# A list schedule of a decoder layer's token mixers with measured task times, and five gate tiles among its filler

## The chip, the cores and the metric

One core of a Trainium2 chip runs the whole layer as one launch. The metric is the device time of a run in microseconds (us), the median of several runs. The engines are named as in the profile: PE (TensorE matmul), PEld (its weight load), DVE (VectorE), ACT (ScalarE), POOL (GpSimd), SP (SyncE, which here issues the DMAs).

## The reference

```python
for i in range(DEPTH):                      # DEPTH 1, x is 512 x 1024
    h = h + FFN_HALF * _swiglu(_rmsnorm(h, norm_ffn1[i]), ffn1_gate[i], ffn1_up[i], ffn1_down[i])
    u = _rmsnorm(h, norm_mix[i])
    (nq, kc, vc, ksl, vsl, kwn, vwn, ng, sq, sk, sv, ga, gb) = jnp.split(u @ w_in[i], pts, axis=-1)
    ...
    o_a = _nsa(nq, kc, vc, ksl, vsl, kwn, vwn, ng, positions, ...)   # 8 heads: compressed, selected, window
    o_b = _banded_attention(sq, sk, sv, SWA_WINDOW, swa_sinks[i]).reshape(B, S, SWA_Q_W)
    merged = jax.nn.sigmoid(ga) * (o_a @ w_branch_a[i]) + jax.nn.sigmoid(gb) * (o_b @ w_branch_b[i])
    h = h + merged @ w_out[i]
    h = h + FFN_HALF * _swiglu(_rmsnorm(h, norm_ffn2[i]), ffn2_gate[i], ffn2_up[i], ffn2_down[i])
return _rmsnorm(h, norm_final)
```

## The kernel before

Every matrix product is made of three matmuls in fp32r: each weight block and each activation is split into a high part and a low part (`whi`, `wlo`; `uh`, `ul`). A weight block (`raw`, 128 rows x 8 x 128) comes by DMA from the SP queue into one of four raw buffers; ACT writes `whi` (L93) and DVE or POOL writes `wlo` (L97, "a split"). Both go into a ring of four slots. A split in halves is 128x512.

The stages are: first FFN, mixers, merge, second FFN. In the mixers (`layer`, from the line `plan = Schedule(...)`) all steps are tasks: projections of `u` (`project`, 256 columns for two weight blocks at a time), their ropes and transposes, the compression of keys and values (`compress`), and the attention of 8 sliding-window units and then 24 units of the sparse attention (`attend`: scores on PE, mask and minimum on DVE, exponentials on ACT, "weighing" of the probabilities by the inverse sum on DVE or POOL, transposes and value products on PE). Each attention step is a chain over PE, DVE and ACT.

The matmuls of projections and compression are *filler* (`filler`, rank 9000): they stand in one chain on PE, and the schedule puts them where PE has no attention step to do. Behind the projections the filler goes on with the tiles of the merge gates that depend on `u` alone (`gate_early`): eight tiles of gate A and `GB_EARLY` tiles of gate B. A gate tile is 24 matmuls of 512 columns; its result is copied by ACT to `turn_a` and written to DRAM (`zd`) from the SP queue.

`Schedule.run` (L199) is the planner, and it runs while the program is built: of all ready tasks it takes the one with the smallest key, adds its time in us to the clock of its engine, and emits its instructions. A task may name two engines with a time for each. A buffer ring (`Ring`) holds a task back until a buffer is free by the plan. What it makes is a fixed order of instructions on each engine; on the chip an engine waits wherever an instruction's input is late.

The merge then goes over eight tiles `d`: it loads the stored gate tiles (`load_z`, a DMA and a product by `r_b` on POOL), computes those tiles of gate B that are not stored (24 matmuls and a product on DVE), makes the two branch products (12 matmuls each), multiplies on DVE, adds on POOL, and splits the sum for the product with `w_out`.

## Time and profile before

| | |
|---|---|
| runs | 1142.55, 1146.53, 1146.96 us, median 1146.53 |
| profiled execution | 1143.02 us, of which the span of its instructions is 1141.3 us |
| PE busy | 1117.3 us, 98% of the span |
| DVE, ACT, POOL busy | 652.8, 440.9, 132.1 us |
| mixers | from about 388 to 640 us of the span |
| merge, with the product with `w_out` | from 640 us |

A matmul is shown from its start to the modelled end of its pipeline, while the next one starts before that end. So a PE that is shown as busy is not always at its peak, and a short wait can lie within the busy time. The table of stretches gives the busy time of each engine within a stretch and the granted share of TensorE's clock (PEclk).

### The profile page before, as it was taken

How to read it: one execution, taken by the hardware profiler on the slowest of the kernel's cores; microseconds unless marked ns; L12 is line 12 of the kernel's file. 1: busy time of each engine (PE TensorE's matmuls, PEld its weight loads, DVE VectorE, ACT ScalarE, POOL GpSimd, SP SyncE). 2: the span in 40 equal slices, each digit the busy share in tenths (PEclk: the TensorE clock that was granted, in tenths of full speed). 3: DMA queues.
4: the chain of work that ended last, by engine and by line, in shares of the span. 5: the costliest groups of instructions: out<-in, count | busy, mean ns of one | idle time of the engine just before them, and what ended most of it. 6: DMA issues, size and time to landing. Idle time of an engine off the chain costs nothing.

```text
span 1141.3 us, 14617 instructions
## 1 busy us (share of the span) xinstructions
PE 1117.3 (98%) x5583; PEld 939.8 (82%) x5583; DVE 652.8 (57%) x1227; ACT 440.9 (39%) x858; POOL 132.1 (12%) x137
## 2 busy tenths in 40 slices
PE   8999999999999999999999899999999999999997
PEld 6888888888888999888888688888888888888875
DVE  4564345643547599999889644565443344433453
ACT  4432122321323356757777533333222133222432
POOL 0100000000005221422112222240000000000001
PEclk9999999999999999999999999999999999999999
DMA  7233333233225442333111345423333332333221
GB/s 226 76 111 111 92 93 111 78 107 111 74 84 155 131 111 76 83 103 84 47 38 37 101 134 157 139 88 116 97 110 94 92 101 84 111 93 92 75 73 74
DMA packets 198287, 113.34 MB, mean 99 GB/s; under 512 B 4996, under 2 KB 191944, under 8 KB 198216
## 3 DMA queue, kind: packets, MB, share of 16 engines
q1 hardware_dynamic: 197416, 111.33, 34.0%
q8 instruction: 44, 0.72, 0.3%
q10 hardware_dynamic: 800, 1.07, 0.3%
q14 instruction: 27, 0.22, 0.1%
HBM read 105.83 MB, written 6.55 MB: 98 GB/s over the span
## 4 chain that ended last, share of the span: by engine, by line
PE 88%; DVE 8%; issue 1%; ACT 1%; DMA 0%; SPq 0%; POOLq 0%; DVEq 0%; ACTq 0%
PE acc L250 32%; PE s L250 28%; PE o L250 25%; DVE wlo L97 2%; PE tp L1244 2%; DVE s L1150 1%; DVE pts L1259 1%; PE tp L250 0%; DVE osum L1287 0%; DVE pbuf L1181 0%; PE tp L870 0%; DVE h L504 0%; DVE pbuf L1179 0%; DMA w_in<-in_ffn_up_dram 0%; PE tp L1365 0%
## 5 line engine op out<-in xcount | busy, mean ns | idle before, releaser
L97 DVE TENSOR_TENSOR wlo<-raw,whi 128x1024 fp32r<-128x1024 f32 (+3 forms) x221 | 242.6, 1127 | 28.3 <-ACT whi L93 27.3
L93 ACT CAST whi<-raw 128x1024 fp32r<-128x1024 f32 (+3 forms) x223 | 189.8, 890 | 131.2 <-PE acc L250 53.8
L250 PE MATMUL acc<-uh,whi 128*128 128x512 f32 x296 | 117.1, 396 | 0.0
L250 PE MATMUL acc<-ul,whi 128*128 128x512 f32 x296 | 115.7, 391 | 0.0
L250 PE MATMUL acc<-uh,wlo 128*128 128x512 f32 x296 | 115.7, 391 | 0.0
L250 PE MATMUL s<-uh,whi 128*128 128x512 f32 x280 | 109.4, 391 | 0.0
L250 PE MATMUL s<-ul,whi 128*128 128x512 f32 x280 | 109.2, 390 | 0.0
L250 PE MATMUL s<-uh,wlo 128*128 128x512 f32 x280 | 109.0, 389 | 0.0
L250 PE MATMUL o<-uh,whi 128*128 128x512 f32 x256 | 101.2, 395 | 0.6 <-ACT uh L553 0.6
L250 PE MATMUL o<-ul,whi 128*128 128x512 f32 x256 | 100.1, 391 | 0.0
L250 PE MATMUL o<-uh,wlo 128*128 128x512 f32 x256 | 99.8, 390 | 0.0
L253 ACT CAST G<-g 128x512 fp32r<-128x512 f32 x44 | 27.3, 621 | 186.2 <-DVE g L469 186.2
L250 PE MATMUL acc<-G,whi 128*128 128x512 f32 x280 | 87.6, 394 | 0.0
L250 PE MATMUL s<-G,whi 128*128 128x512 f32 x228 | 70.3, 389 | 0.0
L250 PE MATMUL o<-G,whi 128*128 128x512 f32 x228 | 70.2, 389 | 0.0
L250 PE MATMUL acc<-whi,uh 128*128 128x256 f32 x224 | 64.7, 289 | 2.0 <-DVE v L829 2.0
L250 PEld LDWEIGHTS acc<-uh,wlo 128*128 128x128 f32 x296 | 55.6, 188 | 12.3 <-DVE wlo L97 0.4
L250 PE MATMUL acc<-wlo,uh 128*128 128x256 f32 x224 | 63.6, 284 | 1.6 <-DVE wlo L97 1.6
L465 ACT ACTIVATE s<-z 128x512 f32<-128x512 f32 x44 | 27.9, 633 | 95.7 <-DVE z L463 95.7
L250 PEld LDWEIGHTS acc<-uh,whi 128*128 128x128 f32 x296 | 55.7, 188 | 10.8 <-issue 0.2
L250 PEld LDWEIGHTS acc<-ul,whi 128*128 128x128 f32 x296 | 55.8, 188 | 10.6
L250 PE MATMUL acc<-whi,ul 128*128 128x256 f32 x224 | 63.3, 283 | 0.0
(298 smaller groups left out, 2115.3 us busy)
## 6 DMA issues: line engine op xcount, KB each, us to landing
raw<-in_ffn_gate_dram SPq DMA_DIRECT2D x42, 512.0 KB, 3.9
raw<-in_ffn_up_dram SPq DMA_DIRECT2D x42, 512.0 KB, 5.1
raw<-in_ffn_down_dram SPq DMA_DIRECT2D x38, 512.0 KB, 4.3
raw<-in_w_in_dram SPq DMA_DIRECT2D x32, 512.0 KB, 4.7
raw<-in_w_out_dram SPq DMA_DIRECT2D x8, 512.0 KB, 4.5
raw<-in_ffn_down_dram SPq DMA_DIRECT2D x8, 384.0 KB, 4.0
zd<-turn_a SPq DMA_DIRECT2D x9, 256.0 KB, 2.1
z<-zd SPq DMA_DIRECT2D x9, 256.0 KB, 2.6
```

Of the source, the lines that this page charges most:

```text
L93: self.nc.scalar.copy(self.place(i)[0][:, k0:k1], self.raw[i][:, k0:k1])
L97: engine.tensor_tensor(lo, self.raw[i][:, k0:k1], f32(hi), op=OP.subtract)
L250: tensor.matmul(out, lhsT, rhs, start=start, stop=stop)
L253: scalar.copy(hi, src)
L465: scalar.activation(s, z, AF.Silu)
L1150: vector.tensor_tensor_reduce(b.view[:, j], b.view[:, j], u.mask, 1.0, u.least(hd), OP.add, OP.min, u.m[:, hd:hd + 1])
L1244: tensor.transpose(ps[:w, hd], u.p[:, hd, kb * w:kb * w + w], ident)
L1259: vector.tensor_tensor(p.lo, flat(b.ps)[:w], f32(p.hi), op=OP.subtract)
```

## The change

The planner's time for nearly every task is replaced, by values that are mostly longer. The fixed delay of 0.15 us between engines becomes one that depends on the engine that comes before and on whether POOL comes after. The key of the choice was "end by the plan, less the task's time on its faster engine"; it is now the start by the plan, then the rank, then the task's time, so that a task with two engines goes to the one that is free first. And gate B's tiles 0, 2, 4, 6 and 7 are filler of the mixers, where it was tile 0 alone; tiles 1, 3 and 5 stay in the merge. No arithmetic changes.

```diff
-GB_EARLY = 1
+GB_EARLY = 0, 2, 4, 6, 7
...
-    SEM = 0.15
+    SEM = {"pe": 0.2, "act": 0.05, "dve": 0.05, "pool": 0.08, "sp": 2.0}
+    TO_POOL = 0.1
...
-                least = min(t.us.values())
                 for e, us in t.us.items():
-                    start = max(at, self.clock[e])
-                    key = (start + us - least, t.rank, t.seq)
+                    start = max(at, self.clock[e], *(end + self.delay(p, e) for p, end in t.sources))
+                    key = (start, t.rank, us, t.seq)
...
-    plan_in(C_GB, GB_EARLY * 128)
+    for d in GB_EARLY:
+        plan_in(C_GB + d * 128, 128)
...
-                    x = prepped[i, half] = task(either(us), low, (t, last_low[0] if half else None), rank=PREP)
+                    x = prepped[i, half] = task(either(us, 0.16), low, (t, last_low[0] if half else None), rank=PREP)
...
-        for d in range(KD + GB_EARLY):
+        for d in (*range(KD), *(KD + d for d in GB_EARLY)):
             gate_early(d)
...
-                    x = task(("act", per * (0.24 + u.n * 0.83e-3)), lambda u=u, hs=hs, b=b: exps(u, hs, b), (x,),
+                    x = task(("act", per * (0.24 + u.n * 1.08e-3)), lambda u=u, hs=hs, b=b: exps(u, hs, b), (x,),
...
-                if d >= GB_EARLY:
+                if d not in GB_EARLY:
                     gates_z[1] = mp.tile([128, S], F32, name="z1")
...
-                elif d + 1 < GB_EARLY:
+                if d + 1 in GB_EARLY:
                     zb = load_z(KD + d + 1)
```

Three places show how the order moves. The rows name output and inputs with their buffer numbers; the line numbers of the changed kernel are four or five higher.

DVE, at the projection of the first keys and values (`acc_3423` before, `acc_3496` now): `turn_a` and `turn_b` are its rope, and `v` is the last step that reads its PSUM bank. Before:

```order
L764 TENSOR_TENSOR turn_a_3574<-acc_3423,cos_87 128x256
L767 TENSOR_TENSOR turn_b_3575<-acc_3423,sin_88 128x4x32 x2
L97 TENSOR_TENSOR wlo_71<-raw_3325,whi_70 128x512
L97 TENSOR_TENSOR wlo_71<-raw_3342,whi_70 128x512
L97 TENSOR_TENSOR wlo_71<-raw_3325,whi_70 128x512
L1287 TENSOR_TENSOR osum_3621<-o_3529,up_3566 64x256 x2
L97 TENSOR_TENSOR wlo_71<-raw_3342,whi_70 128x512
L829 SCALAR_TENSOR_TENSOR v_2556<-acc_3423,rcol_2635,v_2556 128x2x64 x2
```

Now:

```order
L769 TENSOR_TENSOR turn_a_3664<-acc_3496,cos_87 128x256
L772 TENSOR_TENSOR turn_b_3665<-acc_3496,sin_88 128x4x32 x2
L787 TENSOR_TENSOR turn_a_3664<-turn_a_3664,turn_b_3665 128x256
L834 SCALAR_TENSOR_TENSOR v_2556<-acc_3496,rcol_2635,v_2556 128x2x64
L834 SCALAR_TENSOR_TENSOR v_2556<-acc_3496,rcol_2635,v_2556 128x2x64
```

Four splits and an `osum` that stood between the rope and `v` are gone from there; the second half of the rope (L787), which POOL did, is on DVE.

POOL, in the projections, behind the four steps of `compress_in` (`ql` and `G<-osum` are low parts, as `wlo` is). Before:

```order
L861 TENSOR_TENSOR ql_3023<-turn_a_2993,ql_3023 128x8x64
L782 TENSOR_TENSOR turn_a_3025<-turn_a_3025,turn_b_3026 128x512
L97 TENSOR_TENSOR wlo_71<-raw_3078,whi_70 128x512
L861 TENSOR_TENSOR ql_3367<-turn_a_3293,ql_3367 128x8x64
L1292 TENSOR_TENSOR G_76<-osum_3397,G_76 128x256
L782 TENSOR_TENSOR turn_a_3435<-turn_a_3435,turn_b_3436 128x256
L782 TENSOR_TENSOR turn_a_3574<-turn_a_3574,turn_b_3575 128x256
L1179 TENSOR_SCALAR pbuf_2560<-pbuf_2560,c_3499 128x256 x4
```

Now:

```order
L866 TENSOR_TENSOR ql_3250<-turn_a_3223,ql_3250 128x8x64
L1297 TENSOR_TENSOR G_76<-osum_3288,G_76 128x256
L97 TENSOR_TENSOR wlo_71<-raw_3081,whi_70 128x512 x2
L97 TENSOR_TENSOR wlo_71<-raw_3103,whi_70 128x512
L97 TENSOR_TENSOR wlo_71<-raw_3133,whi_70 128x512
L1297 TENSOR_TENSOR G_76<-osum_3467,G_76 128x256
L1184 TENSOR_SCALAR pbuf_2560<-pbuf_2560,c_3345 128x256 x2
L97 TENSOR_TENSOR wlo_71<-raw_3372,whi_70 128x512 x2
L97 TENSOR_TENSOR wlo_71<-raw_3393,whi_70 128x512
L97 TENSOR_TENSOR wlo_71<-raw_3418,whi_70 128x512 x2
```

Splits of weights have taken the place of rope sums and weighings on POOL: over the whole program POOL has 30 half splits where it had 2, and DVE 50 where it had 70 (eight more halves come with the gate tiles). Of the weighings in blocks of 384 and 512 columns, POOL keeps 1 of 20.

PE, at the end of the mixers: `o` with `pts` are value products, `tp` transposes of probabilities, `acc` with `uh` or `ul` filler, and `acc` with `G` the first branch product of the merge. Before:

```order
L250 MATMUL acc_5635<-uh_74,wlo_71 128x512
L1244 MATMUL tp_5796<-ident_79,pbuf_2560 128x128 x4
L250 MATMUL o_5808<-pts_2561,v_2556 128x512 x2
L1244 MATMUL tp_5813<-ident_79,pc_5742 32x128 x4
L250 MATMUL o_5808<-pts_2561,v_2556 128x512 x2
L250 MATMUL o_5808<-pts_2561,vc_2549 128x512
L250 MATMUL acc_5852<-G_76,whi_70 128x512 x2
```

Now (from the same last-but-one transposes on; then follow eight more filler matmuls and `acc_5988<-G`):

```order
L254 MATMUL acc_5891<-uh_74,wlo_71 128x512
L1249 MATMUL tp_5930<-ident_79,pc_5850 32x128 x4
L254 MATMUL acc_5891<-uh_74,whi_70 128x512
L254 MATMUL acc_5891<-ul_75,whi_70 128x512
L254 MATMUL acc_5891<-uh_74,wlo_71 128x512
L254 MATMUL o_5905<-pts_2561,v_2556 128x512 x2
L254 MATMUL acc_5891<-uh_74,whi_70 128x512
L254 MATMUL acc_5891<-ul_75,whi_70 128x512
L254 MATMUL acc_5891<-uh_74,wlo_71 128x512
L254 MATMUL o_5905<-pts_2561,vc_2549 128x512
L254 MATMUL acc_5891<-uh_74,whi_70 128x512
```

The filler had run out before the last five steps of the attention; now three filler matmuls stand between each two of them and nine behind the last.

## Rows read from the trace of the kernel before

**Rows 1.** The page's first part: busy time, share of the span, instructions.

```profile
PE 1117.3 (98%) x5583; PEld 939.8 (82%) x5583; DVE 652.8 (57%) x1227; ACT 440.9 (39%) x858; POOL 132.1 (12%) x137
```

**Rows 2.** Busy time by stretch: its length, then each engine (instructions), PEclk, DMA.

```profile
core 0: us, PE busy (x) PEld busy (x) DVE busy (x) ACT busy (x) POOL busy (x), PEclk, DMA share, GB/s
388.00:520.00 132.00, 126.46 (x1039) 122.85 (x1038) 120.21 (x338) 87.22 (x239) 32.57 (x32) 1.00 0.34 89
520.00:630.00 110.00, 109.96 (x606) 90.34 (x604) 98.05 (x299) 80.72 (x244) 22.75 (x32) 1.00 0.18 53
630.00:640.00 10.00, 6.87 (x31) 4.10 (x30) 7.90 (x25) 6.26 (x23) 2.90 (x3) 1.00 0.24 81
640.00:650.00 10.00, 10.00 (x38) 8.17 (x38) 4.80 (x7) 5.01 (x8) 3.05 (x3) 0.83 0.32 105
```

**Rows 3.** PE's waits from 388 to 645 us: total, times, longest.

```profile
PE o L250 <- DVE pts L1259: 2.1, 3, 0.9
PE acc L250 <- DVE v L829: 2.0, 1, 2.0
PE acc L250 <- DVE wlo L97: 1.6, 2, 1.0
...
PE tp L250 <- DVE sqacc L995: 0.6, 2, 0.4
```

**Rows 4.** PE in order of time: start, length, matmul, [idle before, releaser].

```profile
457.04 0.28 PE L250 MATMUL acc<-whi,G 128*128 128x256 f32 x1
457.16 0.28 PE L250 MATMUL acc<-wlo,G 128*128 128x256 f32 x1
459.49 0.36 PE L250 MATMUL acc<-whi,uh 128*128 128x256 f32 x1 [2.05 <-DVE v L829]
...
636.13 0.49 PE L250 MATMUL o<-pts,v 128*128 128x512 f32 x1 [0.91 <-DVE pts L1259]
...
639.52 0.50 PE L250 MATMUL o<-pts,vc 64*128 64x512 f32 x1 [0.92 <-DVE pts L1259]
639.95 1.22 PE L250 MATMUL acc<-G,whi 128*128 128x512 f32 x2
...
643.67 0.63 PE L250 MATMUL acc<-G,whi 128*128 128x512 f32 x2
...
647.09 0.39 PE L250 MATMUL s<-uh,whi 128*128 128x512 f32 x1
647.32 0.39 PE L250 MATMUL s<-ul,whi 128*128 128x512 f32 x1
```

**Rows 5.** DVE in order of time, ahead of PE's longest wait.

```profile
454.90 2.43 DVE L97 TENSOR_TENSOR wlo<-raw,whi 128x512 fp32r<-128x512 f32 x3
457.26 0.84 DVE L1287 TENSOR_TENSOR osum<-o,up 64x256 f32<-64x256 f32 x2
...
458.74 0.60 DVE L829 SCALAR_TENSOR_TENSOR v<-acc,rcol,v 128x128 fp32r<-128x128 f32 x2
```

**Rows 6.** DVE's groups by shape, 388 to 640 us: busy us, mean ns of one.

```profile
L97 DVE TENSOR_TENSOR wlo<-raw,whi 128x512 fp32r<-128x512 f32 x56 | 42.9, 816 | 2.7 <-ACT whi L93 2.6
...
L1181 DVE TENSOR_SCALAR pbuf<-pbuf,c,gate 128x512 f32<-128x512 f32 x7 | 3.8, 547 | 0.3
...
L1181 DVE TENSOR_SCALAR pbuf<-pbuf,c,gate 128x384 f32<-128x384 f32 x5 | 2.4, 480 | 0.3
```

**Rows 7.** DVE's splits (L97), 388 to 641 us: ns min/median/max.

```profile
L97 DVE TENSOR_TENSOR wlo<-raw,whi x60: 411/682/1799, 388.8 to 601.8; 128x512 fp32r<-128x512 f32 x56, 128x256 fp32r<-128x256 f32 x4
```

**Rows 8.** POOL's groups by shape, 388 to 720 us.

```profile
L1319 POOL TENSOR_TENSOR z<-z,r_b 128x512 f32<-128x512 f32 x9 | 11.8, 1306 | 31.8 <-DMA z<-zd 18.4 <-DVE z L1332 12.4 <-PE tp L1244 1.0
...
L97 POOL TENSOR_TENSOR wlo<-raw,whi 128x512 fp32r<-128x512 f32 x2 | 2.6, 1320 | 16.6 <-ACT whi L93 16.6
```

**Rows 9.** POOL's waits, 370 to 660 us: total, times, longest.

```profile
POOL G L1292 <- ACT G L1291: 41.0, 7, 16.8
```

**Rows 10.** The page's DMA issues: KB each, us to landing.

```profile
z<-zd SPq DMA_DIRECT2D x9, 256.0 KB, 2.6
```

More of the change, by code (lines that the diff above doesn't have):

```diff
@@ L221, in run @@
                 n.left -= 1
-                n.ready = max(n.ready, end + (0.0 if e in n.us and len(n.us) == 1 else self.SEM))
+                n.sources.append((e, end))
+                n.ready = max(n.ready, end)
                 if n.left == 0:
@@ L751, in emit @@
                                 mm(ps[:, t], ul[:, j, ts], hi[:, :, j], False, j == KD - 1)
-                        x = filler(0.65, emit, (prepped[first, k // 4], prepped[first + 1, k // 4]),
+                        x = filler(0.725, emit, (prepped[first, k // 4], prepped[first + 1, k // 4]),
                                    take=[(r_acc, b)] if t == 0 and k == 0 else ())
@@ L831, in v_low @@
                                                     op0=OP.mult, op1=OP.subtract)
-                v_ready[ty, t0] = task(("dve", 0.5), v_low, (x1, vh), give=[(r_acc, b)], rank=-1)
+                v_ready[ty, t0] = task(("dve", 0.6), v_low, (x1, vh), give=[(r_acc, b)], rank=-1)
                 def dup():
@@ L870, in turn @@
                             tensor.transpose(p[:, hd], s.ql[:, t, hd], ident_r)
-                    tt = task(("pe", 0.25), turn, (lo,), take=[(r_tp, bank)],
+                    tt = task(("pe", 0.33), turn, (lo,), take=[(r_tp, bank)],
                               give=[(r_ql, key)] if t else (), rank=-1)
                     q_ready[slot0 + t0 + t] = task(
-                        ("act", 0.5), lambda t=t, bank=bank: scalar.copy(G[:, slot0 + t0 + t], f32(flat(bank.ps))),
+                        ("act", 0.59), lambda t=t, bank=bank: scalar.copy(G[:, slot0 + t0 + t], f32(flat(bank.ps))),
                         (tt, *wait), give=[(r_tp, bank)], rank=-1)
@@ L963, in emit @@
                         mm(ps, blk[ix][:, r * 8 + i], lo[:, :, i], False, i == 7)
-                x = filler(0.43, emit, (prepped[first, j // 4], prepped[first + 1, j // 4], *ins),
+                x = filler(0.48, emit, (prepped[first, j // 4], prepped[first + 1, j // 4], *ins),
                            take=[(r_acc, b)] if j == 0 else ())
@@ L987, in poly @@
                 vector.tensor_tensor(gy, gy, gx, op=OP.mult)
-            x = task(("dve", 1.0), poly, (x,), give=[(r_tp, bank)], rank=-1)
+            x = task(("dve", 1.6), poly, (x,), give=[(r_tp, bank)], rank=-1)
             x = task(("act", 0.25), lambda: scalar.activation(gy, gy, AF.Tanh, scale=math.sqrt(2 / math.pi)), (x,),
@@ L995, in product @@
                 vector.scalar_tensor_tensor(gy, gy, 1.0, gx, op0=OP.add, op1=OP.mult)
-            x = task(("dve", 0.5), product, (x,), rank=-1)
+            x = task(("dve", 0.7), product, (x,), rank=-1)
             bank2 = Bank()
@@ L1055, in emit @@
                     mm(ps, lo[:, k], uh[:, k], False, k == KD - 1)
-                x = filler(0.65, emit, (prepped[first, k // 4],), take=[(r_acc, b)] if k == 0 else ())
+                x = filler(0.685, emit, (prepped[first, k // 4],), take=[(r_acc, b)] if k == 0 else ())
             used[first] = x
@@ L1062, in out @@
                 nc.sync.dma_start(zd[d], z)
-            x = task(("act", 0.5), out, (x,), take=[(r_turn, b)], give=[(r_acc, b)], rank=-1)
+            x = task(("act", 0.6), out, (x,), take=[(r_turn, b)], give=[(r_acc, b)], rank=-1)
             task(("sp", 2.0), lambda: None, (x,), give=[(r_turn, b)], rank=-1)
@@ L1259, in low @@
                         vector.tensor_tensor(p.lo, flat(b.ps)[:w], f32(p.hi), op=OP.subtract)
-                    hi = task(("act", 0.5), high, (t_last,), rank=rank, take=[(r_pt, p)])
-                    lo = task(("dve", 0.62), low, (hi,), rank=rank, give=[(r_tp, b)])
+                    hi = task(("act", 0.59), high, (t_last,), rank=rank, take=[(r_pt, p)])
+                    lo = task(("dve", 0.69), low, (hi,), rank=rank, give=[(r_tp, b)])
                     def value(u=u, kb=kb, p=p):
@@ L1270, in value @@
                         mm(o, u.v(kb), p.lo, False, kb == u.nb - 1 and u.last)
-                    v_last = task(("pe", 0.22 if u.ty == 2 else 0.43), value, (v_last, lo, *u.v_ready), rank=rank,
+                    v_last = task(("pe", 0.42 if u.ty == 2 else 0.455), value, (v_last, lo, *u.v_ready), rank=rank,
                                   give=[(r_pt, p)],
@@ L1320, in load_z @@
                 return z
[L1322 removed]
+            za, zb = load_z(0), load_z(KD)
             for d in range(KD):
@@ L1327, in layer @@
                     za = load_z(d + 1)
-                if d >= GB_EARLY:
+                if d not in GB_EARLY:
                     gates_z[1] = mp.tile([128, S], F32, name="z1")
```

33 lines of the change are left out of this document (17 added, 16 removed).

## The prediction

> **What bounds the kernel now.** I began with the page's first part: PE is busy for 1117.3 of 1141.3 us [rows 1], so no change that only moves work can bring more than some 24 us, and moving matmuls from the merge into the mixers moves as much PE time as it takes away. What is to be had are PE's waits, and the second question is where they lie. The stretches answer it [rows 2]: PE is idle for 132.00 - 126.46 = 5.54 us in the projections (388 to 520 us), 0.04 us in the 110 us of sparse attention behind them, and 3.13 us in the last 10 us of the mixers; and in the 10 us after that the granted clock is 0.83. In the projections DVE is busy for 120.21 of 132 us, 91%. Then the list of waits [rows 3]: seven lines, 11 waits, 8.5 us in sum, and every one of them is put down to DVE. So the mixers are held up by DVE, off and on, in a stage that PE would otherwise set.
>
> How much that costs is read from the starts of matmuls [rows 4]. Filler matmuls of 256 columns start 0.12 us apart (457.04, 457.16) though each is shown for 0.28; the next one starts at 459.49, which is 2.33 - 0.12 = 2.21 us late where the row says 2.05. Each wait is thus some 0.16 us longer than its row, 1.8 us for 11 of them. The clock: the nine matmuls of 512 columns from 639.95 to 643.67 take 3.72 us, while at full clock they start 0.23 apart (647.09, 647.32), which makes 2.05; so 1.67 us are lost there at the lower of the two levels, 1.2 GHz, after three waits of 0.9 us each in the 4 us ahead. The sum of all that can be won is 5.54 + 0.04 + 3.13 + 1.8 + 1.67 = 12.2 us, of it some 6.8 in the projections and 5.3 at the end. Waits shorter than 0.16 us show in no row; I allow 2 us for them at the low end of the range, nothing in the sum.
>
> **The change part by part.** *The longest wait.* PE waits at 457.16 for the PSUM bank that the step `v` frees, and DVE got to `v` late: between the rope and `v` stood three splits (2.43 us), an `osum` pair (0.84) and a fourth split [rows 5], about 4 us of work. In the new order one rope sum stands there instead, as the rows of DVE's order ahead show. That wait, 2.2 us, should go. It is what the longer task times do: the old plan had DVE far ahead of where the chip has it, and put splits in its way that the chip could not do in that time.
>
> *DVE's load.* In the new order DVE has 20 half splits fewer (50 for 70): 20 x 0.816 = 16.3 us less [rows 6]. It takes over 11 weighings of 384 columns and 8 of 512 from POOL: 11 x 0.480 + 8 x 0.547 = 9.7 us more [rows 6], nearly all in the sparse attention; and some ten smaller ones, in the sliding-window units, at no more than 0.48 each, 4.8 us at most. Of the extra splits on POOL about 20 stand in the projections. So DVE's work there goes from 120.2 to about 120.2 - 16.3 + 4.8 = 109 us of at least 126.5 us of PE work, 86% at most. In the sparse attention it goes from 98.05 + 7.90 to some 116 us, but there PE's stretch grows by four gate tiles of 24 matmuls at 0.227 us (2.05 / 9), 21.8 us, from 120 to 142: 82%. In the stretch from 520 to 630 us DVE was at 98.05 of 110, 89%, and PE idle for 0.04 us [rows 2]. Both stretches would now be below that.
>
> *What stays of the 6.8 us in the projections.* Bounds: nothing (as in the stretch at 89%), and all of it, if DVE were still late at each place. I take 1.5 us, much nearer to the first since the share falls below that row's.
>
> *The end of the mixers.* Before, the filler had run out, and the last steps stood back to back on PE. Now 3 filler matmuls (0.68 us) stand between each two of the last steps, and 9 (2.04 us) behind the last one. The three waits of 0.9 us there [rows 3, 4] shrink to 0.24 each, 0.7 us in all; without waits I see no reason for the clock to fall, so its 1.67 us go too. What is late next is the first use of the last unit's `G`: 12 matmuls of the other branch stood ahead of it before and no wait is listed there [rows 3]; now 21 do. I keep 0.7 of the 5.3 us (bounds 0 and, if the attention ends 2 us later than planned so that filler runs dry again, 3).
>
> *The four gate tiles.* 96 matmuls of 512 columns leave the merge and enter the mixers: zero. Each brings an ACT copy and a 256 KB write on SP's queue, and in the merge a load and a product on POOL (1.306 us [rows 8]) for a product that DVE no longer does; none of them is work of PE. SP's queue stands in order: a write waits for its copy, and weight loads stand behind it, but these run three blocks (over 8 us of PE work) ahead. In the merge a tile whose gates are both stored takes PE 24 x 0.227 = 5.45 us. Tiles 6 and 7 come one after the other: tile 7's gates are loaded only when tile 5 is split, in 2.6 us [rows 10]; then two POOL products (2.6 us) stand ahead of the sums of tiles 6 and 7 on POOL's queue (estimated at a product's 1.3 each), and a split on ACT and DVE ends it (estimated at twice 0.68): 9.2 us behind tile 5's split, which by the same values comes some 3.4 us behind its last branch product. PE runs on through 10.9 us of branch products and 21 matmuls of `w_out` (4.8 us) before it needs tile 7's sum: 15.7 against 12.6. Bounds 0 and 3 us, if the locks told of below hit each step; I take 0.
>
> *Waits that are new.* 28 more half splits stand on POOL, at 1.320 us each where DVE's median is 0.682 [rows 7, 8]. PE's filler waits for both. A split is made two to four blocks ahead; a pair of blocks feeds 96 matmuls of a projection, 11.5 us. That covers 0.64 us, but the blocks of `compress` feed 16 matmuls, 1.9 us, for four half splits. Bounds 0 and 0.64 x 20 = 13 us; I take 0.5.
>
> Sum: 12.2 - 1.5 - 0.7 - 0 - 0.5 = 9.5 us, and 1143.0 - 9.5 = 1133.5 us on the scale of the profiled execution. The runs shown lie from 0.5 below to 3.9 above that execution; I take 1134.
>
> **A rule that speaks against it.** Where a DVE split met a POOL sum it took up to 1.799 us for a median of 0.682 [rows 7], and the mean of all 56 is 0.816 [rows 6], 7.5 us in sum. The Trainium skill, SBUF — State Buffer, section "Who interferes with whom", says that a DVE instruction with two SBUF inputs and a GpSimd instruction that reads SBUF lock each other out for a whole instruction. By that rule the longest split of the trace is one that waited out a POOL sum, and each of the new POOL splits can do the same to DVE. What that would give is the first rival.
>
> **The rivals.** *POOL's splits take back what DVE gains.* A split that is held up loses 1.799 - 0.682 = 1.1 us [rows 7]. If each of the 20 extra POOL splits in the projections costs DVE that much, its work there is 109 + 22 = 131 us, over the 128 us or so that the stretch would take, and it is the bound again: the 6.8 us stay, the end is still won (4.6), and 0.5 to 1 us of late splits comes on top. 1143.0 - 4 = 1139. For it: rows 7. Against it: over all 56 splits the mean lies only 0.13 us above the median [rows 6, 7], so most did not meet a POOL step at its start.
>
> *The schedule only moves the waits.* The plan has no lock in it and its times are means; DVE is late at other steps, and the filler that was to cover the end is used up earlier. Then half of 12.2 us is won: 1137. Against it: where DVE's share was 89% there was no wait.
>
> *Slower: splits queued behind POOL's `G` steps.* POOL works in order, and it waited 41.0 us for ACT ahead of seven `G` steps, 16.8 at the longest [rows 9]. In the new order ten such steps are on POOL and splits stand right behind most of them. If an attention unit ends late, the splits behind its `G` step are late, and with them PE's filler, which ends later units. At 2 us (as the wait at 457 us) for each of eight of them, 16 us come back: 1143.0 - 12.2 + 16 + 1.5 = 1148. It decides from 9.5 us in sum, 1.2 for each. Against it: the splits run blocks ahead of their use.
>
> **How the numbers follow.** Forecast 0.70 (1129 to 1137); POOL's splits 0.14 (1139); moved waits 0.10 (1137); slower 0.06 (1148). The low end is all 12.2 us and 2 us of hidden waits: 1129, less 1 since a run can lie below the profiled one; the high end takes in the first two rivals and the runs' scatter of 3.9 us: 1143. About 0.5%, 5.7 us, is what a measurement of this kernel can tell from no change. Against the median of 1146.53 that is 1140.8, against the profiled execution 1137.3. All of the forecast and half of the moved waits come out as faster, 0.76 with a bit of the first rival; the rest of these two as the same, 0.18; slower 0.06.
>
> **What would show it.** Right: PE's idle time from 388 to 520 us below 2 us, no wait of 2 us for `v`; the granted clock 1.00 in each stretch up to the merge; the filler's last matmuls behind the last value product with waits of under 0.3 us; DVE's share below 88% in the projections; the merge without a wait of PE. Wrong: waits of PE for POOL's splits; DVE's mean split over 0.9 us; a wait of PE at `w_out` for `mh`; or waits of PE for DVE as long as before at other steps.

## The result, and the profile after

The changed kernel takes 1156.16 us (median of 4 runs, 1155.72 to 1156.53) where the kernel before takes 1146.62; the ratio is 1.0091, with a 95% interval of 1.0068 to 1.0114. It is slower, by 0.9%, where 1134 us and faster was forecast. The profiled execution took 1155.72 us, its span is 1154.0 against 1141.3 [rows 1]: 12.7 us to be found.

The page's first part after the change, busy time, share of the span and instructions, which answers to [rows 1]:

```profile
PE 1121.1 (97%) x5583; PEld 940.9 (82%) x5583; DVE 663.9 (58%) x1226; ACT 442.1 (38%) x866; POOL 157.4 (14%) x142
```

Five stretches of it: length, then busy time of each engine (instructions), granted clock, DMA share, GB/s. They answer to [rows 2]; with four more gate tiles among the filler the mixers now end at about 665 us, not at 641.

```profile
388.00:520.00 132.00, 121.10 (x985) 116.22 (x984) 116.61 (x306) 80.02 (x214) 47.39 (x36) 1.00 0.33 89
520.00:660.00 140.00, 139.37 (x759) 115.06 (x758) 126.14 (x358) 98.21 (x298) 28.55 (x30) 1.00 0.21 63
...
670.00:680.00 10.00, 6.09 (x16) 4.10 (x15) 3.15 (x5) 3.39 (x6) 4.98 (x4) 0.67 0.35 118
680.00:730.00 50.00, 50.00 (x221) 41.17 (x220) 25.56 (x36) 18.16 (x32) 19.50 (x15) 1.00 0.58 172
730.00:740.00 10.00, 8.02 (x28) 5.86 (x27) 4.83 (x6) 4.78 (x7) 2.95 (x3) 0.83 0.79 231
```

PE is idle for 10.90 us in the projections, where it was 5.54; the merge has two holes, at 670 and at 730 us, each with a lower granted clock. PE's waits from 388 to 790 us (total, times, longest), which answer to [rows 3]:

```profile
PE acc L254 <- DVE wlo L97: 3.9, 4, 1.6
PE s L254 <- ACT whi L93: 3.9, 1, 3.9
PE tp L254 <- DVE sqacc L977: 1.7, 2, 1.5
PE tp L1249 <- DVE c L1173: 1.6, 1, 1.6
PE o L254 <- ACT whi L93: 1.5, 1, 1.5
PE acc L254 <- DVE v L834: 1.4, 1, 1.4
PE tp L807 <- ACT pbuf L911: 1.3, 1, 1.3
...
```

Two kinds make up most of it: waits for DVE in the projections as before, only more, and waits for ACT's weight casts (`whi`), which were not there. No row of PE names a split on POOL; its weight load (PEld) waited for one twice, 2.4 us in all.

Since such rows miss the slow clock behind a wait, this text measures PE's **lost time**: for each matmul, the time to the next one's start less what its shape takes at full clock (0.230 us for 512 columns, 0.121 for 256, 0.110 for all others), summed by stage. The 32 matmuls of 384 columns need more than 0.110, which puts the same 2.0 us into each row of the column of the mixers; differences are free of it. The stages are the projections (388 to 520 us), the rest of the mixers (up to the first matmul of the merge that reads `G`), the merge (up to the first that reads `mh`), and `w_out`. The expectations below count the end of the mixers from 620 us on: 5.3 before, 2.7 after the change, 21.2 with the schedule alone. The last two columns are counts of POOL's instructions from 388 to 680 us; `osum` is the start of the last `osum` on DVE, which is where attention ends.

```
kernel             time us  ratio   lost: proj. mixers merge w_out   osum  POOL splits, weighings
before             1146.6   -              5.5   10.2   0.7   0.5    641       2     42
after              1156.2   1.0091        12.5    6.7   7.8   3.0    664      32     13
e1_sched_only      1167.7   1.0196        12.4   25.3   0.4   0.5    664      28     10
e2_gates_only      1150.4   1.0045         7.3    6.4   8.0   1.9    648       3     43
e3_dve_splits      1164.0   1.0158         7.0   23.2   3.9   3.1    679       0      8
e4_next_first      1153.3   1.0061        15.0    6.7   3.2   1.9    668      32     13
e5_old_key         1166.0   1.0183        16.9   17.7   3.0   3.1    682      13      5
e6_gates_clean     1140.0   0.9956         5.6    6.4   1.1   1.6    646       3     43
e7_after_clean     1147.9   1.0032        12.5    6.8   1.0   1.6    665      32     13
e8_beside_tt       1154.3   1.0078        15.1   10.9   1.2   0.5    652       2     42
e9_beside_set      1144.0   0.9987         4.8   10.5   0.7   0.5    640       2     42
e11_same_delay     1157.7   1.0116        20.0    9.9  -0.5   0.5    656      28     52
e12_weigh_dve      1160.7   1.0143         8.9   22.7   1.6   0.5    658       5      0
e13_before_pool    1159.8   1.0125        22.9   10.0   1.1   0.5    659      22     30
e14_emit_dve       1156.2   1.0090        11.5    6.9   8.6   3.1    664       0     13
e15_all_three      1140.1   0.9964         6.7    5.4   0.1   1.6    656       0     64
```

Ratios are to the runs of before on the same chip; their intervals are no wider than 0.0046. After less before is 7.0 in the projections, -3.5 in the rest of the mixers, 7.1 in the merge and 2.5 at `w_out`: 13.1 us, and -0.3 in the first FFN, against 12.7 of span.

### The profile page after: what moved, and what is told of

The parts are those of the page before. It is cut to its first block, busy times and chain, and to the rows that moved or that the text cites. A ratio compares the mean times of both kernels' runs of the same rounds, so it can differ in the third digit from the quotient of the medians.

```text
span 1154.0 us, 14622 instructions
## 1 busy us (share of the span) xinstructions
PE 1121.1 (97%) x5583; PEld 940.9 (82%) x5583; DVE 663.9 (58%) x1226; ACT 442.1 (38%) x866; POOL 157.4 (14%) x142
## 4 chain that ended last, share of the span: by engine, by line
PE 86%; DVE 8%; ACT 3%; issue 1%; DMA 1%; POOL 0%; SPq 0%; POOLq 0%; DVEq 0%; ACTq 0%
PE acc L254 31%; PE s L254 26%; PE o L254 26%; DVE wlo L97 3%; PE tp L1249 2%; ACT whi L93 1%; DVE s L1155 1%; DVE pts L1264 1%; PE tp L254 0%; DVE pbuf L1184 0%; ACT pbuf L1163 0%; DVE turn_b L772 0%; DVE turn_a L769 0%; DMA z<-zd 0%; DVE h L509 0%
## 5 line engine op out<-in xcount | busy, mean ns | idle before, releaser
L97 DVE TENSOR_TENSOR wlo<-raw,whi 128x1024 fp32r<-128x1024 f32 (+3 forms) x195 | 231.2, 1209 | 30.2 <-ACT whi L93 29.1
L254 PE MATMUL acc<-uh,whi 128*128 128x512 f32 x352 | 139.9, 397 | 0.0
L254 PE MATMUL acc<-uh,wlo 128*128 128x512 f32 x352 | 137.6, 391 | 0.0
L254 PE MATMUL acc<-ul,whi 128*128 128x512 f32 x352 | 137.5, 391 | 0.0
L254 PE MATMUL s<-uh,whi 128*128 128x512 f32 x232 | 91.9, 396 | 3.9 <-ACT whi L93 3.9
L254 PE MATMUL s<-ul,whi 128*128 128x512 f32 x232 | 91.5, 394 | 0.0
L254 PE MATMUL s<-uh,wlo 128*128 128x512 f32 x232 | 91.3, 394 | 0.0
L254 PE MATMUL s<-G,whi 128*128 128x512 f32 x268 | 82.6, 389 | 0.0
L254 PEld LDWEIGHTS acc<-uh,wlo 128*128 128x128 f32 x352 | 66.1, 188 | 14.6 <-DVE wlo L97 0.6
L254 PEld LDWEIGHTS acc<-uh,whi 128*128 128x128 f32 x352 | 66.3, 188 | 13.1 <-issue 0.7
L254 PEld LDWEIGHTS acc<-ul,whi 128*128 128x128 f32 x352 | 66.3, 188 | 12.6
L254 PE MATMUL acc<-G,whi 128*128 128x512 f32 x232 | 71.4, 389 | 0.0
```

What stands on the lines that cost most here:

```text
L97: engine.tensor_tensor(lo, self.raw[i][:, k0:k1], f32(hi), op=OP.subtract)
L254: tensor.matmul(out, lhsT, rhs, start=start, stop=stop)
```

## The hole at the start of the merge

ACT of the changed kernel in order of time (start, length, line, [idle before, releaser]) from 664 to 676 us, then POOL, SP's queue and PE there:

```profile
665.56 0.59 ACT L1066 COPY turn_a<-acc 128x512 f32<-128x512 f32 x1 [0.29 <-PE acc L254]
666.16 1.28 ACT L1341 ACT_TABLE_LOAD   x1
673.21 0.63 ACT L1341 ACTIVATE z<-z 128x512 f32<-128x512 f32 x1 [5.76 <-POOL z L1324]
673.75 1.03 ACT L93 CAST whi<-raw 128x1024 fp32r<-128x1024 f32 x1
```

```profile
670.70 3.71 POOL L1324 TENSOR_TENSOR z<-z,r_b 128x512 f32<-128x512 f32 x3 [10.81 <-DMA z<-zd]
```

```profile
666.17 0.32 SPq L1067 DMA_DIRECT2D zd<-turn_a  x1
666.60 2.16 SPq L1323 DMA_DIRECT2D z<-zd  x2
```

```profile
670.57 0.39 PE L254 MATMUL o<-G,wlo 128*128 128x512 f32 x1
674.83 0.79 PE L254 MATMUL s<-uh,whi 128*128 128x512 f32 x1 [3.87 <-ACT whi L93]
675.42 0.63 PE L254 MATMUL s<-ul,whi 128*128 128x512 f32 x1
676.09 0.79 PE L254 MATMUL s<-uh,wlo 128*128 128x512 f32 x1
...
677.11 0.63 PE L254 MATMUL s<-ul,whi 128*128 128x512 f32 x1
677.53 0.63 PE L254 MATMUL s<-uh,wlo 128*128 128x512 f32 x1
```

Read it from the top. The last stored gate tile now ends the mixers: its copy stands at 665.56 us and its write at 666.17, behind the merge's first matmul, where before the copy (633.87) was 6 us ahead of that matmul (639.95 [rows 4]). The merge's first load of a gate tile stands behind that write on SP's queue; POOL's products follow at 670.70 and the first sigmoid at 673.21. None of that is what PE needs: the next matmul wants a weight block whose cast is written behind the sigmoid in ACT's order, and so ACT sits idle for 5.76 us ahead of a cast whose input is there. Behind the wait three matmuls start some 0.6 us apart and the next ones 0.43, not 0.23: the granted clock, 1.00 up to 672 us, is 0.50 from 674 to 680. Something like it stands at 731 us:

```profile
727.88 2.55 POOL L1324 TENSOR_TENSOR z<-z,r_b 128x512 f32<-128x512 f32 x2 [4.28 <-DVE z L1344]
730.39 1.29 POOL L1346 TENSOR_TENSOR z<-z,z 128x512 f32<-128x512 f32 x1
```

```profile
731.71 0.62 ACT L257 CAST mh<-z 128x512 fp32r<-128x512 f32 x1 [5.36 <-POOL z L1346]
732.24 0.62 ACT L1341 ACTIVATE z<-z 128x512 f32<-128x512 f32 x1
732.77 1.03 ACT L93 CAST whi<-raw 128x1024 fp32r<-128x1024 f32 x1
```

Here POOL's sum for tile 6 stands behind the two products for tile 7, whose loads were issued at 725.01, right behind the split (724.29) that is the last to read tile 5's buffer. ACT waits for that sum ahead of its `mh` cast, and the weight cast for `w_out` stands behind this cast and a sigmoid of tile 7.

## The experiments

**One part of the change at a time.** The schedule alone has `GB_EARLY = 0,` in the changed kernel. The other kernel has the planner, key and times of before with the tuple below and the loops that read it:

```diff
-GB_EARLY = 1
+GB_EARLY = 0, 2, 4, 6, 7
```

> The new list schedule alone: GB_EARLY holds only tile 0, as before the change, so gate tiles 2, 4, 6 and 7 are computed in the merge again. Theory, two separate causes: (1) the new order puts the weight splits on POOL and costs TensorE about 7 us in the projections (idle of 388 to 520 us 10.9 against 5.5 before); (2) the five early gate tiles cost two waits in the merge and at w_out, 7.1 and about 4 us, because weight casts stand behind sigmoids on ACT, while they win the waits at the end of the mixers, 6.6 us. With (1) alone the projections keep an idle time of 10 to 12 us, the two waits in the merge are gone, and the end of the mixers waits again as before or more: 1156 - 11 + 6.6 = 1152 us (1149 to 1155). Rival, the gate tiles carry the whole loss: 1142 to 1147.

> The five early gate tiles alone, with the planner and the task times of before. By the theory of two causes the projections idle 5 to 6 us as before, the waits at the end of the mixers go (6.6 us) and the two waits of the merge and of w_out are as after the change (11 us): 1146.6 + 11 - 6.6 = 1151 us (1148 to 1154). Rival, the loss is all in the new order: 1138 to 1142.

The schedule alone took 1167.7 us, beyond both theories; the gates alone 1150.4, as the theory of two causes had it. The table shows why the first missed: attention ends at 664 us with the new schedule whether the gate tiles are in it or not, 23 us later than before. Without them filler is out early and PE loses 25.3 us in the rest of the mixers; with them 22 us of gate matmuls (four more tiles, 96 matmuls at 0.23) lie over just that delay. One half of the change hides what the other costs, and a comparison of before and after alone would not have shown it.

**The merge.** First the next block ahead of the sigmoid:

```diff
                 for z, x in zip(gates_z[::-1], (b_in, a_in)):
+                    w = W.next()
                     scalar.activation(z, z, AF.Sigmoid)
                     ps = acc(False)
-                    mm3(ps.rearrange("p (t c) -> p t c", t=4), W.next(), x, 4)
+                    mm3(ps.rearrange("p (t c) -> p t c", t=4), w, x, 4)
```

> The changed kernel with one edit in the merge loop: the next weight block's cast and split are written ahead of the sigmoid instead of behind it. Theory, in ACT's order the casts stand behind sigmoids that wait for the stored gate tiles: the waits of 3.9 us at 670 us with its slow clock after it (7.1 together) and of about 4 us at w_out go or fall below 1.5 each, 1156 - 9 = 1147 us (1145 to 1150). Rival, TensorE waits there for the transfers and products of the gate tiles themselves, or for the weight loads behind them: the waits move by a product or two and the time stays at 1154 to 1157.

Then with `bufs=3` for the tiles `z0` and `z1` as well, once on the changed kernel and once on the gate tiles with the planner of before:

> The changed kernel with both edits of the merge: the next block's cast and split ahead of each sigmoid, and three buffers for z0 and z1. With the first edit alone (1153.3 us) two waits of about 2.3 us each were left where a cast stands behind a sigmoid whose gate tile came late. Theory, the load starts late because a buffer comes free late: both go, 1153.3 - 4 = 1149 us (1147 to 1151), which is before plus the 7 us of the projections minus what the end of the mixers gave. Rival, the loads are late by the queue and the transfers: 1152 to 1154.

> The five gate tiles with the planner of before, the next block's cast and split written ahead of each sigmoid in the merge, and three buffers instead of two for z0 and z1. Theory of the merge: of the 9.9 us that TensorE waits there with two buffers and the old place (8.0 in the merge, 1.9 at w_out) casts behind sigmoids are the cause, and the sigmoids wait for gate tiles whose load starts only when a buffer comes free: 1 to 3 us are left, 1150.4 - 8 = 1142.5 us (1140 to 1145), faster than both kernels. Rival, the transfers themselves are late in the merge (they moved 183 GB/s there against 150 before): 1147 us or more.

The first edit took the wait at 670 us away; merge and `w_out` together lost 5.1 us in place of 10.8. The total won only 2.9 us, so that 1153.3 lies between its two ranges: this execution lost 2.5 us more in the projections, where the granted clock fell to 0.89 from 430 to 460 us, 200 us ahead of the edit and with the same waits there as in the changed kernel. With the buffers it is 2.6, and the time 1147.9, within its expectation. With the planner of before it is 1140.0, faster than both kernels, than the one before by 0.4% (ratio 0.9956, interval 0.9942 to 0.9970). PE's waits behind 645 us in the four kernels with gate tiles, in the order e2_gates_only, e4_next_first, e7_after_clean, e6_gates_clean:

```profile
PE s L250 <- ACT whi L93: 4.1, 1, 4.1
PE o L250 <- ACT whi L93: 1.6, 1, 1.6
PE o L250 <- DVE wlo L97: 0.5, 1, 0.5
```

```profile
PE o L254 <- ACT whi L93: 2.8, 2, 1.5
PE o L254 <- DVE wlo L97: 1.1, 2, 0.5
...
```

```profile
PE o L254 <- DVE wlo L97: 1.3, 3, 0.8
...
```

```profile
PE o L250 <- DVE wlo L97: 1.2, 3, 0.5
```

The rows for ACT go from two waits of 5.7 us to none. The rival, transfers that are late by themselves, is out: in e6_gates_clean the stretch from 670 to 720 us moved 192 GB/s, more than the 172 of the changed kernel's, and PE was busy for 49.01 of 50 us:

```profile
670.00:720.00 50.00, 49.01 (x214) 39.47 (x213) 29.98 (x38) 20.87 (x36) 22.25 (x17) 1.00 0.63 192
```

Each edit has its own wait: with the cast alone the one at `w_out` stayed (1.36 us for 1.46) and one of 1.49 us came up at 692 us, each ahead of a weight cast behind an `mh` cast; both went with the third buffer.

**What delays the end of attention.** First the planner's key alone as before:

```diff
+                least = min(t.us.values())
-                    key = (start, t.rank, us, t.seq)
+                    key = (start + us - least, t.rank, t.seq)
```

> The changed kernel with one line of the planner as before: a task and its engine are chosen by start + us - least, then rank, and not by start first; the new task times and the five early gate tiles stay. The runs so far: with the new schedule the last osum of the mixers stands at 664 us with or without the early gates, with the old schedule at 641 and, with the five gates, at 648 us. Theory, the key does it: by 'start first' a weighing always goes to DVE, which has just made its factor c and so can start it 0.15 us sooner than POOL, and the weight splits go to POOL. With the old key POOL makes about 40 weighings and few splits again, the mixers end at 645 to 652 us, and the time is that of the five gates with the old planner, 1150 us (1147 to 1153). Rival, the task times do it: the mixers still end beyond 658 us and the time is 1155 to 1160.

It missed: 1166.0 us, attention ends at 682. The key alone is not it. But the table's last column agrees with the reason given, the weighings: POOL made 5 of them here, 13 after the change, 42 before. What sends them to DVE is neither key nor times but `delay`: a weighing's input `c` comes from DVE, which may start at once by the plan, while POOL sees it 0.05 + 0.1 us later. The next kernel takes that away in the schedule alone, and the one behind it lets the planner of the kernel before put the weighings on DVE alone:

```diff
-                    start = max(at, self.clock[e], *(end + self.delay(p, e) for p, end in t.sources))
+                    start = max(at, self.clock[e], *(end + (self.delay(p, e) if len(t.us) == 1 else 0.15)
+                                                     for p, end in t.sources))
```

> The new schedule alone (one early gate tile, 1167.7 us in its own run) with one more edit: a task that may go to DVE or POOL sees its inputs 0.15 us late on either engine, as in the planner of before, where the change lets DVE see a result of DVE at once and POOL 0.15 us later. By the order of its instructions POOL then makes 52 weighings (10 in the new schedule alone, 42 before) and still 28 weight splits. Theory, the weighings that moved from POOL to DVE make the mixers end 23 us later: the last osum goes from 664 us back to 641 to 650, TensorE's waits at the end of the mixers from 21 to 5 or 6 us, the projections keep their 12 us of idle time, and the time is 1152 us (1149 to 1156). Rival, the task times or the splits on POOL delay the mixers: the last osum stays beyond 655 us and the time is 1161 or more.

```diff
-                        x = task({"dve": per * (0.2 + u.n * 0.55e-3),
-                                  "pool": per * (0.26 + u.n * (3.4e-3 if u.ty == 3 else 1e-3))},
-                                 lambda e, u=u, hs=hs: weigh(u, hs, engine[e]), (x,), rank=rank)
+                        x = task(("dve", per * (0.2 + u.n * 0.55e-3)),
+                                 lambda u=u, hs=hs: weigh(u, hs, vector), (x,), rank=rank)
```

> The kernel before with one edit: the weighings of p may only be planned on DVE (in the kernel before 42 of them are on POOL and 54 on DVE). Theory, it is the weighings' engine that decides when the mixers end: DVE gets about 19 us more (42 at some 450 ns), the last osum goes from 641 to 655 us or later, TensorE's waits ahead of the merge from 5 to 18 us or more, and the time is 1158 us or more (1156 to 1168). Rival, DVE has room for them (it was busy 229 of 253 us up to the last osum): the last osum stays within 4 us of 641 and the time within 4 us of 1146.

The second came out on the theory's side: with no weighing on POOL, under the old planner, the mixers behind the projections lose 22.7 us in place of 10.2. The first lies between the ranges, 1157.7 us and attention's end at 656, yet the stage in question did what the theory said: with 52 weighings on POOL it loses 9.9 us in place of 25.3, as before the change. What spoils the total is the projections, 7.6 us more than in the schedule alone; they lose 14.5 more than before, and attention ends 14.6 later than before, so behind them no delay is left. Why they lose more is open. The rows of `osum` on DVE (count, ns min/median/max, first and last start), for before, e1_sched_only, e11_same_delay and e12_weigh_dve:

```profile
L1287 DVE TENSOR_TENSOR osum<-o,up x32: 397/417/420, 441.5 to 641.2; 64x256 f32<-64x256 f32 x32
```

```profile
L1292 DVE TENSOR_TENSOR osum<-o,up x32: 405/417/419, 437.6 to 664.0; 64x256 f32<-64x256 f32 x32
```

```profile
L1292 DVE TENSOR_TENSOR osum<-o,up x32: 396/417/418, 434.5 to 655.8; 64x256 f32<-64x256 f32 x32
```

```profile
L1286 DVE TENSOR_TENSOR osum<-o,up x32: 404/417/420, 442.5 to 658.1; 64x256 f32<-64x256 f32 x32
```

The last number of each is what to read: 641, 664, 656, 658.

**The projections.** First the splits planned on DVE alone (`either(us, 0.16)` becomes `("dve", us + 0.16)`):

> The changed kernel with one edit: the weight splits may only be planned on DVE. Theory, the splits on POOL are what costs in the projections: TensorE's idle time of 388 to 520 us falls from 10.9 to 5 or 6, a 128x512 split on DVE from a mean of 1051 ns to about 800, the weighings from 596 and 616 to about 547 and 480; the merge stays as it was; 1156 - 5.5 = 1150.5 us (1148 to 1153). Rival, the new order itself (start first, rank second): idle time and total stay, 1155 to 1157. Second rival, DVE gets too full by the 30 splits of 0.8 us that come back (24 us): 1158 to 1165.

The stage did what the theory said, lost time 7.0 for 12.5 us and DVE's splits back near 0.8 us, and the total went the other way: attention ended at 679 us, and the 1164.0 us are in the second rival's range. Its reason, DVE's load, does not carry them: up to the last `osum` DVE was busy for 248.5 us here, against 245 in the changed kernel and in e14_emit_dve below, where DVE also makes every split and nearly as many weighings and attention ends at 664. So the order of this plan must be what delays attention; by which step is open. Next, work on POOL that nobody waits for, in the kernel before, behind every second planned split; and as much queue time or less without a read:

```diff
+                            for _ in range(4):
+                                gpsimd.tensor_tensor(scr, scr, scr, op=OP.add)
```

> The kernel before with work added on POOL: behind every second planned weight split four tensor_tensor of 128x128 on a scratch tile, about 1.4 us, which nobody reads or waits for; nothing else is moved. Theory, an operation of POOL that reads two operands holds DVE up for its length, whoever waits for its result: DVE's 128x512 splits go from a mean of 816 to about 1000 ns, TensorE's idle time of 388 to 520 us from 5.5 to 9 or more, and the time to 1151 us (1149 to 1156). Rival, only what waits for POOL's late results loses: DVE's durations stay, and the time is that of the next run, which fills POOL with memsets.

```diff
+                            for _ in range(5):
+                                gpsimd.memset(scr, 0.0)
```

> The kernel before with five memsets of 128x128 on POOL behind every second planned weight split, about 1.4 us, on a scratch tile that nobody reads. POOL's queue is as full as in the run with tensor_tensor, but these operations read nothing. Theory of the lock: DVE's durations stay as before (splits 816 ns within 40), the time at 1146 to 1149 us. Rival, lateness: the weighings and subtractions of POOL come later by what stands ahead of them, and the time is that of the run with tensor_tensor within 1 us.

POOL's rows for the added work and DVE's row for the 128x512 splits from 388 to 640 us (busy us, mean ns), first with tensor_tensor, then with memset:

```profile
L714 POOL TENSOR_TENSOR scr<-scr 128x128 f32<-128x128 f32 x110 | 58.3, 530 | 7.2
L97 DVE TENSOR_TENSOR wlo<-raw,whi 128x512 fp32r<-128x512 f32 x56 | 44.8, 849 | 1.8 <-ACT whi L93 1.8
```

```profile
L714 POOL MEMSET scr<- 128x128 f32 x135 | 28.0, 207 | 6.7
L97 DVE TENSOR_TENSOR wlo<-raw,whi 128x512 fp32r<-128x512 f32 x56 | 41.7, 795 | 2.6 <-ACT whi L93 2.5
```

The memsets cost nothing (1144.0 us, under the range, with DVE's splits as long as expected). The others cost 8.6 us, but not in the expected way: DVE's splits went from 816 [rows 6] to 849 ns only, and the largest new waits of PE are two for a `ql` that POOL made late:

```profile
PE tp L877 <- POOL ql L868: 5.9, 2, 3.3
```

The pair is not clean either, since a group of tensor_tensor took POOL 2.1 us and one of memsets 1.0. It shows that short reading steps on POOL make POOL late; that they hold DVE up, it shows only weakly. So two more runs: one keeps the planner of before and moves splits to POOL, one keeps the new order and takes them off. In the planner of before, a split on POOL is made cheap up to the end of the projections:

```diff
+        price = [1.1]          # set to 2 ahead of the gate tiles
-                    x = prepped[i, half] = task(either(us), low, ...
+                    x = prepped[i, half] = task({"dve": us + 0.06, "pool": price[0] * us + 0.1}, low, ...
```

> The kernel before with one price changed in its planner: up to the end of the projections a weight split on POOL counts as 1.1 times its task time and 0.1 us, not twice. By the order of its instructions POOL then makes 22 splits (19 of the changed kernel's stand between 388 and 520 us) instead of 2; key, task times and delays are those of before. Theory, splits on POOL cost DVE about as much as they save it (in the changed kernel 12.6 us of stretched DVE work beside 19 splits, 0.66 us for each, where DVE itself needs 0.68) and come late: the excess of TensorE between 388 and 520 us goes from 5.5 to 10 or more, the time to 1151 us (1149 to 1156). Rival, the new order costs the 7 us there, not the splits on POOL: the time stays within 3 us of 1146.

And in the new order, with the plan left believing that POOL makes 32 of them, every split emitted on DVE:

```diff
-                        W.low(i, k.start, k.stop, engine[e])
+                        W.low(i, k.start, k.stop, vector)
```

> The changed kernel, planned as it is, with every split written on DVE at the place that the plan gave it, POOL's too: 32 splits of 0.68 us (22 us) come back to DVE and 45 us of POOL's work go. The plan doesn't know of it, so the order on every engine is otherwise that of the changed kernel. Theory, a split on POOL holds DVE up by what DVE would need for it: DVE's work and TensorE's waits stay, 1156 us (1152 to 1159). Rival, POOL's splits do relieve DVE: the projections and the end of the mixers lose some 10 us more, 1164 or later. Second rival, POOL's splits are what costs there: the projections' excess falls from 12.5 to 7 us, and the time to 1150.

Under the old planner 20 more splits on POOL (and 12 weighings fewer) took the projections from 5.5 to 22.9 us lost and the time to 1159.8, beyond the theory's range. POOL's splits being late themselves is little of it; PE waits for DVE there:

```profile
PE acc L250 <- DVE v L830: 6.0, 1, 6.0
...
PE acc L250 <- POOL wlo L97: 0.9, 1, 0.9
```

In the new order taking all 32 off POOL changed nothing: 1156.2 us, against 1156.2. DVE's 128x512 splits from 388 to 680 us and the two stretches of the mixers, first of the changed kernel (its stretches are shown above), then of e14_emit_dve:

```profile
L97 DVE TENSOR_TENSOR wlo<-raw,whi 128x512 fp32r<-128x512 f32 x37 | 37.4, 1041 | 2.7 <-ACT whi L93 2.6
```

```profile
L97 DVE TENSOR_TENSOR wlo<-raw,whi 128x512 fp32r<-128x512 f32 x67 | 47.1, 743 | 2.8 <-ACT whi L93 2.6
```

```profile
388.00:520.00 132.00, 123.60 (x995) 118.76 (x993) 116.02 (x326) 80.25 (x215) 19.53 (x17) 0.99 0.34 89
520.00:660.00 140.00, 138.80 (x756) 114.82 (x756) 126.76 (x371) 98.12 (x298) 11.46 (x17) 1.00 0.22 63
```

Add DVE's two stretches: 116.61 + 126.14 = 242.75 us with 32 splits on POOL, 116.02 + 126.76 = 242.78 with none, while POOL's busy time falls from 75.9 to 31.0. A split on POOL saves DVE nothing here. DVE's lost part can be read from the rows at 417 us of the changed kernel, POOL first, then DVE:

```profile
417.24 5.95 POOL L97 TENSOR_TENSOR wlo<-raw,whi 128x512 fp32r<-128x512 f32 x4 [4.42 <-ACT whi L93]
```

```profile
418.15 0.94 DVE L787 TENSOR_TENSOR turn_a<-turn_a,turn_b 128x512 f32<-128x512 f32 x1
419.01 1.78 DVE L97 TENSOR_TENSOR wlo<-raw,whi 128x512 fp32r<-128x512 f32 x1
```

Four POOL splits run back to back, 1.49 us each, and DVE's own split takes 1.78 us where its median was 0.682 [rows 7]. It is not one case: of the 37 splits above, the 15 beside which POOL did nothing took at most 0.69 us, the 22 that overlapped an operation of POOL 1.29 on the mean. Over the projections, DVE's steps that ran beside a POOL split were longer by 12.6 us in sum than the shortest of their form in any trace of before, of after or with the memsets: 12.6 / 19 = 0.66 us for each POOL split there, about DVE's own price for a split, 0.68 (steps that also met another operation of POOL count; without them the sum is 10.0). The run with memsets has 0.6 us of this beside all its memsets. The Trainium skill, SBUF — State Buffer, section "Who interferes with whom", names the pair: a DVE instruction with two SBUF inputs contends with a GpSimd instruction that reads SBUF, not with one that only writes it. These numbers agree with it.

**All three at once.** The changed kernel with its key, its times and its five gate tiles, splits planned on DVE alone, equal delays for both engines, and the merge's two edits:

> The changed kernel with all three suspected causes undone and its key, its task times and its five early gate tiles kept: splits planned on DVE alone, a task that may go to DVE or POOL sees its inputs 0.15 us late on either (64 weighings are then on POOL), and in the merge the next cast ahead of each sigmoid with three buffers for z0 and z1. Theory, these three are the whole loss: TensorE's excess is 5 to 7 us in the projections (12.5 after the change), 1 to 3 at the end of the mixers, 1 in the merge and 1.6 at w_out; the last osum stands at 645 to 655 us, and the time is 1142 us (1138 to 1145), against 1140.0 with the same merge and the planner of before. Rival, there is a fourth cause in the key or the task times: 1148 or more.

1140.1 us (0.9964, 0.9951 to 0.9978), with the lost time as expected in each stage (1.3 at the end of the mixers) and attention's end at 656 us, one beyond its expectation. So the three causes together carry the whole loss, and what is left of the new schedule, start first and measured times, is worth as much here as the old one: 1140.0 in e6_gates_clean against 1140.1. Attention still ends 10 us later than there (646); the filler covers it, and what delays it is open.

## Why the prediction was wrong, step by step

**What bounds the kernel.** Right that PE's waits are what can be won, wrong to stop there. Rows of waits tell where PE waits now, not how long attention's chain over DVE takes. DVE's share was read (91%, 89%) and taken for room; the start of the last `osum` was never asked for, and it moved by 23 us.

**DVE's load** is the step that failed first. It counted 20 splits fewer on DVE as 16.3 us less and got 109 us of work in the projections, 86% at most. Measured: 116.6 of 132 us, 88%, and DVE's mean split at 1041 ns; e14_emit_dve shows that a split on POOL saves DVE nothing. The weighings that come to DVE were counted rightly, 29 of them, at 9.7 + 4.8 us, and set against this gain; with the gain gone they stood alone, and delayed attention (e11_same_delay, e12_weigh_dve). In sum the prediction had DVE's work from 388 us to the end of attention about 2 us down (16.3 against 14.5); it went up by 18, from 227 to 245: the splits gave 9.0 us back, the weighings took 18.2 more, and other steps took the rest.

**What stays in the projections**: 1.5 us taken, between nothing and all of 6.8; 12.5 lost by the measure used here (5.5 before), beyond the upper bound. The bound was made from the waits of before, and left out that a plan which believes in POOL's splits makes an order that DVE can't keep. e13_before_pool and e14_emit_dve show it from both sides: splits put on POOL by the plan cost 17 us under the old planner, and the order that the change made costs nearly the same with the splits back on DVE (11.5 for 12.5); planned without them (e3_dve_splits, e15_all_three) the stage loses 7.0 and 6.7.

**The first rival** was this mechanism with a wrong price. It let the lock take back what DVE gains in the projections alone, 1139 us, and was given 0.14. The argument against it, a mean only 0.13 us above the median over 56 splits [rows 6, 7], was read from a trace in which POOL made two splits; DVE's mean with 32 on POOL is 1041 ns, and the text's own mark of failure was 0.9 us. The price was 0.66 us of DVE for each, not 1.1, but it was paid in both stages, and the delay of attention was no part of the rival.

**The end of the mixers**: the waits there went as forecast, and with them the slow clock at 640 us; the rest of the mixers loses 3.5 us less. But the gate tiles' 22 us went to cover a delay that the schedule made, not the 5 us that were there.

**The four gate tiles**: taken as 0, bounds 0 and 3; measured 9.6 (7.1 + 2.5). Loads, buffers and POOL's sums were followed, PE's time behind them too (15.7 against 12.6 us). Missed were two things that the order shows: ACT's casts of weights are written behind the sigmoids and the `mh` casts, so that whatever delays a gate tile delays weights; and the last stored tile's copy now stands behind the merge's first matmul, and its write on SP's queue directly ahead of the merge's first loads. The late sums of tiles 6 and 7 were foreseen and judged harmless by when PE reads them; the cast behind them was not. What is queued behind a waiting instruction was asked for SP and POOL, not for ACT.

**New waits for POOL's splits**: 0.5 taken, and no wait in the list names them. **The slower rival**, splits behind `G` steps on POOL, did not happen in that form: the sign was its own, the mechanism not.

## What to carry to other kernels

A second engine relieves a first only if the two don't hold each other up: before a planner is given a choice, run the same order once with the choice forced and compare the first engine's busy time. Here an operation with two inputs in SBUF was worth nothing on POOL, while weighings, which scale one tensor, were worth 12 to 15 us of PE's time in the mixers behind the projections (e12_weigh_dve, e11_same_delay; in the second the projections lost 7.6 of it again). That the one input makes the difference was not tested by itself.

When work is moved to cover waits, read first when the covered chain ends, with the work and without it; a change that moves both can look harmless in the stage it damages.

In a queue that is in order, write the instruction that feeds the bottleneck ahead of the one that waits for a transfer: that line and one buffer more gave 8.3 us on the changed kernel and 10.4 on the old planner's, of which PE's lost time in the merge and at `w_out` explains 8.2 and 7.2.

## What the runs showed of the hardware

POOL's own price moved: a 128x512 split took it 1.32 us where it made two [rows 8] and 1.46 us in the changed kernel (388 to 680 us):

```profile
L97 POOL TENSOR_TENSOR wlo<-raw,whi 128x512 fp32r<-128x512 f32 x30 | 43.2, 1459 | 69.9 <-ACT whi L93 63.9 <-PE acc L254 6.1
```

A tensor_tensor of 128x128 took POOL 530 ns beside DVE's work, a memset of the same shape 207.

In a wait of 3.9 us that ended at 674.8 us the granted clock fell from 1.00 (2.4 GHz) to 0.50 (1.2 GHz); it stayed there to 680 us, with matmuls of 512 columns 0.43 us apart. Waits of at most 1.6 us spread over the projections left it at 1.00 in the changed kernel's profiled execution; in that of e4_next_first, with the same waits there, it was 0.86 from 440 to 450 us and 0.79 from 450 to 460. What made the difference is open.
